# Second layer's experts: both parts of the tokens as 128 stationary columns in the gate and up products

## The chip, the cores and the metric

The kernel runs on one core of one Trainium2 chip. The metric is the device time of one launch in microseconds (us), as a median of several runs. The engines are named as the profile names them: PE (TensorE, matmuls), PEld (its loads of the stationary operand), DVE (VectorE), ACT (ScalarE), POOL (GpSimd) and SP (SyncE, which issues most DMAs). Each engine executes its own queue of instructions in order.

## What is computed

The reference is a model of two layers on 256 context and 256 latent tokens of 1024 channels. In each layer four mixers run, their outputs are merged, and a mixture of 16 experts follows, of which each token uses two. The change touches only the experts of the second layer, which treats the 256 latent tokens alone:

```python
def moe_ffn(u, w_group, w_expert, w_gate, w_up, w_down):
    ...
    comb = jnp.sum(jax.nn.one_hot(e_idx, MOE_EXPERTS, dtype=F32) * top_w[..., None], axis=-2).astype(u.dtype)
    y = jnp.zeros_like(u)
    for e in range(MOE_EXPERTS):
        h = jax.nn.silu(u @ w_gate[e]) * (u @ w_up[e])
        y = y + comb[..., e:e + 1] * (h @ w_down[e])
    return y
```

`w_gate` and `w_up` are 1024 x 512 for each expert, `w_down` is 512 x 1024, all float32: 6.3 MB of weights for each of 16 experts.

## The kernel before

**Products in parts.** PE multiplies operands of a rounded float32 type at full speed, so each float32 operand of a large product is split into a high and a low part. `split` (line 298) makes the high part as a copy on ACT (line 299) and the low part as a difference on DVE (line 300). `mm3` (line 320) adds three products: high times high, high times low, low times high. `wsplit` (line 311) loads 1024 columns of weights (512 KB, a tile `raw`) and splits them into `wh` and `wl`. In the expert stage three pairs of buffers take the split weights in turn, so a cast to `wh` waits until PE has finished with the block three before it. The `raw` tiles are a ring of some 21 buffers that SP fills ahead.

**An expert** (`expert`, line 371) has 12 such blocks: four of the gate (`mg`), four of the up (`mup`), four of the down matrix (`mdn`). In the second layer its tokens, at most 64, lie in `xs`: high and low part, channels in partitions, gathered for four experts at a time by products with a selection (`gather`, line 595: tiles `pick`, `uh`, `ul`, result `xx`). For the gate and for the up product, 64 token columns are the stationary operand and 512 weight columns move: two times 24 matmuls. Then ACT takes a Tanh of the gate (line 1403) and DVE makes h in two steps (lines 1404 and 1405; called the first and the second step below). PE transposes h in four pieces (`tr`, line 331), and h is split into `hh` and `hl`. Then 24 matmuls with the down blocks give the output in two halves. ACT scales one half to `yo` (line 1417), DVE the other (line 1418), and POOL writes `yo` to the rows of Y2 in memory by an indirect DMA (line 1419; the trace calls the target Y).

**What is in flight.** The loop over experts is pipelined by generators: three gate blocks of expert e+1 are emitted, then the end of expert e (Tanh, h, transposes, down blocks, `yo`, the write), then the row list of expert e+2 (`entries`, line 1558), then the rest of e+1. `entries` picks the list by small products (`rent,pick`) and DVE puts it into `ri` and `rf` (lines 1575 and 1582). There are four buffers of `ri`, so from the fifth list on, writing `ri` waits until an earlier Y write, which reads its rows from that buffer, has landed. In the program as built that is the write of the `yo` just ahead of it in DVE's queue.

**What sets the order.** A scheduler orders the instructions of every engine when the program is built, by costs of its own. What DVE or PE executes next is therefore fixed, and a late operand stops all that stands behind it.

Of the kernel before, what the change touches and what calls it, by code (L numbers as in the profile page):

```python
# [22 lines left out]
KT = D // 128  # L23
HY0, S50, RW0, M20, GT0, NIN = 0, 768, 1024, 1984, 3016, 7112
# tiles of 128 columns of w_in: Hyena, S5, RWKV (r, k, v, wd | ad), Mamba (z, x, B, C), gates, then gd | dt
# [51 lines left out]
NQS = (2, 4)  # pairs of groups in a part of S5  # L77
# [3 lines left out]
# ---------------------------------------------------------------- constants of the shapes  # L81


def _cst():
# [16 lines left out]
    # N^T of two-token blocks, rows s, columns t; backward scans in partitions 0..63  # L101
# [15 lines left out]
    # places less 1024  # L117
# [3 lines left out]
    # a token's row in U, and in Y2 for its first and second expert; Y2's less that of the rows without a token  # L121
    c["tok"] = np.stack([tok + 1.0, tok, tok + 512.0, tok - 1024.0], 2).reshape(128, 16)
    # resets of the running sums at the ends of 64-token chunks
# [7 lines left out]
def _rows():  # L131
    """rows of the modulation in groups of 32 (context, latent; the bias in the first's third): to each token's stream, to latent"""
    half = np.r_[np.ones(64), np.zeros(64)]
    m = np.zeros((128, 2, 128))
    for p in range(0, 128, 32):
        m[p:p + 2, 0] = half, 1 - half
        m[p + 1, 1] = 1
    m[2] = 1
    return m.reshape(128, 256)
# [39 lines left out]
def pack(inp):  # L179
    """Lays the inputs out for the loads; no arithmetic on them."""  # L180
# [32 lines left out]
    # S5: rows (second index of a pair of groups, state), columns (part, direction, pair)  # L213
# [44 lines left out]
class K:  # L258
# [13 lines left out]
    def pool(self, es, name, bufs=1):  # L272
        """a pool on the side of the parts of a layer"""
        return es.enter_context(self.tc.tile_pool(name=name, bufs=bufs, side="right", reuse_waits="tile"))
# [4 lines left out]
    def stream(self, banks="abgabgab", weights="mggg", parts="mg"):  # L279
        """banks of PSUM and buffers of weights (as loaded, and in parts) that the following program takes in turn:  # L280
        parts of a layer that run beside each other have their own"""
        self.tags, self.wtags, self.ptags = banks, weights, parts or weights
        if RESET:
            self.turn = self.wturn = 0

    def banks(self, **n):
        """the banks of PSUM by tag"""
# [9 lines left out]
    # ---- float32 operands of the large products in two parts of 12 bits: a b = ah bh + al bh + ah bl  # L297
# [4 lines left out]
    def raw(self, ap):  # L302
        """1024 columns of weights"""
# [7 lines left out]
    def wsplit(self, ap, k):  # L311
        """the parts of 1024 columns of weights (k by 1024 / k)"""
# [18 lines left out]
    def tr(self, out, in_, base=0):  # L331
        """out = in_^T on the tensor engine"""
# [6 lines left out]
    def rsqrt(self, pool, out, x, tag):  # L339
        """out = x ** -0.5 by Newton's iteration from the exponent's half; x > 0, small tiles"""  # L340
# [11 lines left out]
    def proj(self, l, t, xm, c0, c1, n=128):  # L352
        """p^T of w_in's tile t: n columns in partitions, tokens c0..c1"""
# [6 lines left out]
    # ------------------------------------------------------------------ RWKV-7  # L360
    def rwkv(self, l, xm, pc, dtT, yT, ctx_out, beside):
        """yT[:, hp, :]: the mixer's output, channels in partitions; columns 0..255 context, 256.. latent.
        dtT: Mamba's dt, from the tile that has both's columns, with tokens in partitions"""
        v, s, g, c = self.v, self.s, self.g, self.c
        with ExitStack() as es:
# [23 lines left out]
            def shifted(ps, n, j, out):  # L389
                """p + (mean of its neighbours - p) mu"""  # L390
# [20 lines left out]
            lo = {0: 64, 1: 0}  # partitions of the solves  # L411
# [4 lines left out]
            own = {d: slice(lo[d], lo[d] + 64) for d in range(2)}  # columns of a direction in the pairs' matrices  # L416
# [8 lines left out]
            for hp in range(2):  # L425
# [3 lines left out]
                # kappa: k k_k over its norm in the head  # L429
# [7 lines left out]
                # block diagonal pairs, of directions or heads: -b~ and k~ against kappa~, and the solves' (later M)  # L437
# [5 lines left out]
                for st in range(2):  # L443
# [6 lines left out]
                    for d in range(2):  # L450
                        dh = 2 * d + hp
                        # decay in log, its running sum in each chunk, and W = exp of that
# [21 lines left out]
                        s.activation(cum, cum, AF.Exp, scale=-1.0)  # 1 / W  # L474
# [16 lines left out]
                        # products of a chunk's tokens, masked: rows k~ and b~ (b~ and k~ backward)  # L491
# [11 lines left out]
                    # (I - N)^-1 of every chunk, N = -tril(kappa~ beta~^T): pairs of blocks, doubling  # L503
# [8 lines left out]
                    def each(a, b, us=range(8)):  # L512
                        """a^T b of the pairs"""
# [18 lines left out]
                    # tokens in partitions: v above (below) the solves, kappa~, and [k~; -b~]  # L532
# [33 lines left out]
                    # per chunk: H' = W_T (M H + k~^T v - b~^T u0), and y's reading of H  # L566
# [15 lines left out]
                    # the states that chunks enter (block diagonal), the last one that of the next stream's first chunk  # L582
# [23 lines left out]
                    # y^T  # L606
# [10 lines left out]
                    # group norm over a head, bonus, gate  # L617
# [24 lines left out]
    def headscale(self, pool, sq, f, eps, is_max, ni):  # L642
        """(f * sum over a head of sq, with eps added or as its least) ** -0.5, over the head's partitions"""
# [18 lines left out]
    # ------------------------------------------------------------------ conv of three taps, channels in partitions  # L662
    def conv3(self, ps, out, w3, b, c0, c1):
        """ps holds columns c0..c1 (of one or both streams)"""
# [8 lines left out]
    def silu(self, x, t):  # L673
        """x = silu(x), with a scratch like it"""
# [4 lines left out]
    # ------------------------------------------------------------------ Mamba-2  # L679
    def mamba(self, es, l, xm, pc, yT, ctx_out, dtT):  # L680
# [4 lines left out]
        if True:  # L685
# [10 lines left out]
            # softplus = max(x, 0) + log1p(exp(-|x|)); log1p(e) = 2 atanh(e / (2 + e))  # L696
# [17 lines left out]
            # running sums within a stream: forward heads 0..3, backward 4..7  # L714
# [16 lines left out]
            # weights of the context's tokens in its last state  # L731
# [6 lines left out]
            for gr in range(2):  # L738
# [8 lines left out]
                # tokens in partitions  # L747
# [10 lines left out]
                # the context's last states, [n, (direction, head, p)]  # L758
# [11 lines left out]
                for st in range(0 if ctx_out else 1, 2):  # L770
                    # C B^T by pairs of tiles, rows j, columns i; masked for each direction
# [33 lines left out]
                # + d x  # L805
                v.scalar_tensor_tensor(yT[:, gr, y0:], X[:, y0:], col("md", gr), py[:, y0:], OP.mult, OP.add)
            # times silu(z), norm over the channels
# [28 lines left out]
    def sin_of(self, pool, out, x, tag, cos=None):  # L836
        """out = sin(x), cos = cos(x): x less its whole turns, taken off in three parts"""
# [20 lines left out]
    def exp_of(self, pool, out, x, tag):  # L858
        """out = exp(x) for small tiles: 2^k times a polynomial of the rest"""
# [13 lines left out]
        # 2^k in two factors  # L873
# [8 lines left out]
    # ------------------------------------------------------------------ Hyena  # L882
    def hyena_filter(self, l, pc, pool, H):
        """H: [frequency, tile, (cos, sin), channel] of the two-sided filters"""
# [87 lines left out]
    # ------------------------------------------------------------------ S5  # L972
    def s5_params(self, l, pool):
        """[state, (part, direction, pair)]: lambda_bar, (lambda_bar - 1) / lambda, the decay over a chunk of
        4 tokens, cos and sin of the angles of a token, and of 1, 2, .. 64 chunks"""
# [44 lines left out]
    def s5_setup(self, l, a, P, tmp, TM, F, TT, ct, R):  # L1020
        """Matrices of 4-token chunks of the pairs of part a: E tokens -> state at the chunk's end, F state that
        enters -> tokens, TT within the chunk; ct: turns of the state by chunk (cos, sin), R: its decay over a chunk."""
# [3 lines left out]
        if True:  # L1026
# [7 lines left out]
            def times(o, x, br, bi, n, conj):  # L1034
                """o = x * b, or the conjugate of (conjugate of x) * b; x, o: [.., re/im, ..]"""
# [927 lines left out]
```

## Time and profile before

| | |
|---|---|
| timed runs | median 2172.78 us (2167.97, 2172.78, 2173.02) |
| span of the profiled execution, first to last instruction | 2165.3 us (its time as a run is not recorded; the timed runs lie 2.7 to 7.7 us above the span) |
| busy, share of the span | PE 91%, PEld 69%, DVE 76%, ACT 46%, POOL 18% |
| mean granted clock of PE | 0.946 of 2.4 GHz |
| moved by DMA | 406.28 MB |
| second layer's experts | about 1836 to 2137 us |

Shares over the whole span say little here, because the kernel has stages with different limits. The stage of the change is read by itself: from the table of 20 us stretches, then from the waits, then from the instructions of DVE and PE in order of time. A matmul's length in the trace includes its way through the array; what a stream of them costs is the distance from start to start.

### The profile page before, as it was taken

What the parts mean: (1) busy time and instruction counts of PE and PEld (TensorE: products, weight loads), DVE (VectorE), ACT (ScalarE), POOL (GpSimd) and SP (SyncE); (2) the same over time, 40 slices, a digit from 0 to 9 for tenths busy, and PEclk for the clock granted to TensorE, in tenths of its full rate; (3) what the DMA queues carried; (4) which work ended last, traced back from release to release, by engine and by line L of the source; (5) the groups of instructions that cost most, each with busy time, mean ns of one, the idle gap of its engine ahead of it and who ended that gap; (6) DMA issues with size and microseconds to landing.
All of it is one profiled execution on the core that took longest, in us unless ns stands there. A gap on an engine that the chain in (4) does not pass through costs nothing. (4 is left out here: it accounts for less than half of the span.)

```text
span 2165.3 us, 31795 instructions
## 1 busy us (share of the span) xinstructions
PE 1970.2 (91%) x11290; PEld 1504.7 (69%) x11290; DVE 1651.0 (76%) x3451; ACT 985.5 (46%) x1571; POOL 399.0 (18%) x502
## 2 busy tenths in 40 slices
PE   6999999889999899999995899899798878999994
PEld 2779889567666678777774689897575767555652
DVE  5575675478888777999996686776879776888895
ACT  3321322244344234777773332323434335777783
POOL 1000100033532322102213010100524221010100
PEclk9999999889999898999998899999898988999997
DMA  7221221533444845999993221312434394899981
GB/s 299 78 74 59 74 67 52 197 123 113 156 146 154 313 172 186 362 368 372 372 341 138 84 90 63 98 52 76 160 134 161 129 350 174 304 329 366 330 325 64
DMA packets 131915, 406.28 MB, mean 188 GB/s; under 512 B 18139, under 2 KB 30205, under 8 KB 131361
## 3 DMA queue, kind: packets, MB, share of 16 engines
q1 hardware_dynamic: 125778, 388.34, 50.6%
q0 software_dynamic: 5968, 15.80, 2.3%
q8 instruction: 92, 1.51, 0.3%
q14 instruction: 77, 0.63, 0.1%
HBM read 374.72 MB, written 34.61 MB: 189 GB/s over the span
## 5 line engine op out<-in xcount | busy, mean ns | idle before, releaser
L299 ACT CAST wh<-raw 128x1024 fp32r<-128x1024 f32 x528 | 553.0, 1048 | 537.9 <-PE bank L337 482.9
L300 DVE TENSOR_TENSOR wl<-raw,wh 128x1024 fp32r<-128x1024 f32 x528 | 642.6, 1231 | 146.4 <-ACT wh L299 143.1
L337 PE MATMUL bank<-xmh,wh 128*128 128x512 f32 (+2 forms) x896 | 338.3, 378 | 15.8 <-ACT wh L299 14.7
L337 PE MATMUL bank<-xmh,wl 128*128 128x512 f32 (+2 forms) x896 | 331.0, 370 | 15.4 <-DVE wl L300 15.4
L337 PE MATMUL bank<-xml,wh 128*128 128x512 f32 (+2 forms) x896 | 326.4, 365 | 0.0
L337 PEld LDWEIGHTS bank<-xmh,wh 128*128 128x128 f32 (+1 forms) x896 | 176.7, 197 | 54.2 <-ACT wh L299 19.2
L337 PEld LDWEIGHTS bank<-xmh,wl 128*128 128x128 f32 (+1 forms) x896 | 175.9, 196 | 51.6 <-DVE wl L300 22.2
L337 PEld LDWEIGHTS bank<-xml,wh 128*128 128x128 f32 (+1 forms) x896 | 176.5, 197 | 29.2 <-issue 6.2
L337 PE MATMUL bank<-wh,xx 128*64 128x512 f32 x512 | 168.1, 397 | 0.2 <-ACT wh L299 0.2
L1419 POOL DMA_INDIRECT Y<-yo,ri x32 | 43.4, 1357 | 420.4 <-DVE yo L1418 304.8
L337 PE MATMUL bank<-DD,TB 128*128 128x64 f32 (+1 forms) x848 | 111.5, 273 | 1.3 <-DVE TB L523 0.9
L337 PEld LDWEIGHTS bank<-DD,TB 128*128 128x128 f32 x848 | 106.3, 192 | 6.0 <-DVE DD L598 0.9
L337 PE MATMUL bank<-wl,xx 128*64 128x512 f32 x256 | 102.8, 402 | 1.3 <-DVE wl L300 1.1
L337 PE MATMUL bank<-wl,hh 128*112 128x512 f32 (+1 forms) x256 | 99.9, 396 | 0.0
L337 PEld LDWEIGHTS bank<-wh,xx 128*64 128x64 f32 x512 | 69.6, 136 | 43.1 <-issue 1.4
L337 PE MATMUL bank<-wl,xh 128*112 128x512 f32 x240 | 97.9, 408 | 0.2
L337 PE MATMUL bank<-wh,hl 128*112 128x512 f32 (+1 forms) x256 | 97.4, 400 | 0.5 <-DVE hl L300 0.2
L337 PE MATMUL bank<-wh,xl 128*112 128x512 f32 x240 | 94.8, 395 | 0.9 <-DVE xl L300 0.9
L337 PE MATMUL bank<-wh,xh 128*112 128x512 f32 x240 | 92.8, 395 | 0.8 <-ACT xh L299 0.8
L337 PE MATMUL bank<-wh,hh 128*112 128x512 f32 (+1 forms) x256 | 89.8, 397 | 1.1 <-ACT hh L299 1.1
L337 PE MATMUL bank<-raw,c 128*32 128x256 f32 x768 | 71.3, 423 | 18.6 <-DMA raw<-in_modw_dram 18.6
L337 PE MATMUL bank<-DD,AB 128*128 128x64 f32 x640 | 84.5, 275 | 0.7 <-DVE DD L510 0.7
(547 smaller groups left out, 3799.5 us busy)
## 6 DMA issues: line engine op xcount, KB each, us to landing
raw<-in_mg_dram SPq DMA_DIRECT2D x128, 512.0 KB
raw<-in_mup_dram SPq DMA_DIRECT2D x128, 512.0 KB
raw<-in_mdn_dram SPq DMA_DIRECT2D x128, 512.0 KB
raw<-in_win_dram SPq DMA_DIRECT2D x112, 512.0 KB
raw<-in_modw_dram SPq DMA_DIRECT2D x96, 512.0 KB
GT<-t SPq DMA_DIRECT2D x32, 256.0 KB
raw<-in_wbr_dram SPq DMA_DIRECT2D x16, 512.0 KB
G<-GT SPq DMA_DIRECT2D x8, 1024.0 KB
```

What stands on the lines that cost most here:

```text
L299: self.s.copy(hi, src)
L300: (eng or self.v).tensor_tensor(lo, src, hi, OP.subtract)
L337: self.t.matmul(out, lhsT=lhsT, rhs=rhs, start=start, stop=stop)
L1419: g.indirect_dma_start(out=Y2, out_offset=bass.IndirectOffsetOnAxis(ap=to, axis=0), in_=yo, in_offset=None, bounds_check=1023, oob_is_err= ...
```

## The change

The two parts of the tokens' operand are stored side by side, so that for each block of 128 channels high and low part form one stationary operand of 128 columns. One product with `wh` then gives high times high in rows 0 to 63 of the bank and low times high in rows 64 to 127; a second one, of the high part alone with `wl`, adds high times low to rows 0 to 63. Two matmuls stand where three stood. ACT copies the two banks of gate and up to SBUF (`gu`), and PE multiplies each 128 x 128 piece of them with two stacked 64 x 64 identities (`i64`). That adds the two halves of rows and transposes in one step, and takes the place of the transposes: eight products for four transposes. Tanh and the two steps on h then run on 128 partitions x 256 columns in place of 64 x 512. The first layer and the overflow loop keep the old path. The diff also drops comments, so line numbers move: 1403 to 1405 become 1423 to 1425, 1418 becomes 1444, 1419 becomes 1445, 1575 and 1582 become 1601 and 1608, and line 1418 of the changed kernel is the new copy.

```diff
+        stacked = OC[l] and xs is not None
...
-        pg, pu = self.bank()[0:cap], self.bank()[0:cap]
+        hh, hl = (tmp.tile([128, 4, cap], F32R, tag="h" + x, bufs=xb[2], name="h" + x) for x in "hl")
+        pg, pu = self.bank(), self.bank()
         for nm, ps in (("mg", pg), ("mup", pu)):
             for kc in range(4):
                 wh, wl = weights(nm, kc, 2)
                 for k in range(2):
                     kk = 2 * kc + k
-                    self.mm3(ps, [z[:, kk] for z in xs], (wh[:, k], wl[:, k]), kk == 0, kk == KT - 1)
+                    if stacked:
+
+                        both = lambda: self.mm(ps, xs[:, kk], wh[:, k], kk == 0, kk == KT - 1)
+                        if kk < KT - 1:
+                            both()
+                        self.mm(ps[0:cap], xs[:, kk, 0:cap], wl[:, k], False, False)
+                        if kk == KT - 1:
+                            both()
+                    else:
+                        self.mm3(ps[0:cap], [z[:, kk] for z in xs], (wh[:, k], wl[:, k]), kk == 0, kk == KT - 1)
                 yield
...
+        if stacked:
+
+            pt = self.bank()
+            for j, ps in enumerate((pg, pu)):
+                r = tmp.tile([128, 512], F32, tag=f"gu{j}", bufs=1, name="gu")
+                s.copy(r, ps)
+                for k in range(4):
+                    self.mm(pt[:, 256 * j + 64 * k:256 * j + 64 * k + 64], r[:, 128 * k:128 * k + 128], self.c["i64"])
+            pg, pu = pt[:, 0:256], pt[:, 256:512]
+            h = tmp.tile([128, 256], F32, tag="h", bufs=xb[1], name="h")
+            s.activation(h, pg, AF.Tanh, scale=0.5)
+            v.scalar_tensor_tensor(h, h, 1.0, pg, OP.add, OP.mult)
+            v.scalar_tensor_tensor(h, h, 0.5, pu, OP.mult, OP.mult)
+            self.split(h.rearrange("p (k t) -> p k t", k=4), hh, hl)
+        else:
...
-                    xx = [tmp.tile([128, KT, 2, 128], F32R, tag="xx", bufs=3, name="xx") for _ in range(2)]
+                    xx = [tmp.tile([128, KT, 2, 2, 64], F32R, tag="xx", bufs=3, name="xx") for _ in range(2)]
...
-                        xs.append([xx[j // 2][:, :, z, 64 * (j % 2):64 * (j % 2) + 64] for z in range(2)])
+                        xs.append(xx[j // 2][:, :, j % 2].rearrange("p k z t -> p k (z t)"))
...
-                            s.copy(xx[j][:, k], ps.rearrange("p (z j t) -> p j z t", z=2, j=2)[:, j])
+                            s.copy(xx[j][:, k], ps.rearrange("p (z j i t) -> p j i z t", z=2, j=2, i=2)[:, j])
```

The scheduler writes the stage in another order with this. DVE, one loop of the middle of the stage, before; `wl` is the low part of a block of weights, `h` the two steps, `yo` the scaled half of the output:

```order
L1418 TENSOR_SCALAR yo<-bank,rf 64x512
L300 TENSOR_TENSOR wl<-raw,wh 128x1024 x2
L1404 SCALAR_TENSOR_TENSOR h<-h,bank 64x512
L300 TENSOR_TENSOR wl<-raw,wh 128x1024 x3
L1405 SCALAR_TENSOR_TENSOR h<-h,bank 64x512
L300 TENSOR_TENSOR wl<-raw,wh 128x1024 x2
L1575 TENSOR_SCALAR ri<-bank 64x1
L1582 COPY rf<-bank 64x1
L300 TENSOR_TENSOR wl<-raw,wh 128x1024
L300 TENSOR_TENSOR hl<-bank,hh 128x256
L300 TENSOR_TENSOR wl<-raw,wh 128x1024 x4
L1418 TENSOR_SCALAR yo<-bank,rf 64x512
```

The same place in DVE's queue in the changed kernel:

```order
L1444 TENSOR_SCALAR yo<-bank,rf 64x512
L300 TENSOR_TENSOR wl<-raw,wh 128x1024 x4
L1601 TENSOR_SCALAR ri<-bank 64x1
L1608 COPY rf<-bank 64x1
L300 TENSOR_TENSOR wl<-raw,wh 128x1024 x4
L1424 SCALAR_TENSOR_TENSOR h<-h,bank 128x256
L300 TENSOR_TENSOR wl<-raw,wh 128x1024
L1425 SCALAR_TENSOR_TENSOR h<-h,bank 128x256
L300 TENSOR_TENSOR hl<-h,hh 128x256
L300 TENSOR_TENSOR wl<-raw,wh 128x1024 x3
L1444 TENSOR_SCALAR yo<-bank,rf 64x512
```

Twelve subtractions stand in each loop both times. The two steps on h moved from the second, fourth and following places to the end, directly ahead of `hl`; three subtractions in place of four stand between `hl` and `yo`; and `ri` moved ahead. Between `yo` and `ri` there are 5, 3, 4, 4, 5, 4, 4, 4, 5, 3, 4 and 4 subtractions in the first twelve loops of the changed kernel, and no `ri` stands in the last three. In before `ri` stands after five subtractions and both steps in the first loop, after 2, 3 and 4 subtractions and the first step in the next three, and from there on ever later, behind the second step.

PE at the transposes of an expert in before (`cst,h`), followed by products of the next expert (`xx`) and the first down products (`hh`, `hl`):

```order
L337 MATMUL bank<-wh,xx 64x512 x2
L334 MATMUL bank<-cst,h 128x64 x4
L337 MATMUL bank<-wl,xx 64x512
L337 MATMUL bank<-wh,xx 64x512 x2
L337 MATMUL bank<-wl,xx 64x512
L337 MATMUL bank<-wh,xx 64x512
L337 MATMUL bank<-wh,hh 64x512 x2
L337 MATMUL bank<-wl,hh 64x512 x2
L337 MATMUL bank<-wh,hl 64x512 x2
```

And at the second four products with `gu` of an expert in the changed kernel:

```order
L337 MATMUL bank<-wl,xx 64x512
L337 MATMUL bank<-wh,xx 128x512
L337 MATMUL bank<-cst,gu 128x64 x4
L337 MATMUL bank<-wl,xx 64x512
L337 MATMUL bank<-wh,xx 128x512
L337 MATMUL bank<-wl,xx 64x512
L337 MATMUL bank<-wh,hh 64x512
L337 MATMUL bank<-wl,hh 64x512
L337 MATMUL bank<-wh,hh 64x512
L337 MATMUL bank<-wl,hh 64x512
L337 MATMUL bank<-wh,hl 64x512 x2
```

Five matmuls stood between the transposes and the first `hh` product; three stand between the last `gu` products and it now, while Tanh, both steps on h and the cast to `hh` come between them on ACT and DVE. SP's and POOL's queues keep their order.

## Rows read from the trace of the kernel before

**Rows 1.** 20 us stretches: length, busy per engine (instructions), granted clock, DMA share, GB/s.

```profile
1900.00:1920.00 20.00, 18.05 (x74) 9.90 (x73) 14.90 (x17) 12.54 (x15) 0.55 (x1) 0.91 0.85 295
...
2060.00:2080.00 20.00, 20.00 (x89) 11.23 (x88) 18.79 (x22) 15.54 (x19) 1.16 (x1) 1.00 1.01 389
```

**Rows 2.** Waits, 1740 to 2140: engine, line, releaser; total us, times, longest.

```profile
ACT wh L299 <- PE bank L337: 74.9, 115, 4.5
...
DVE ri L1575 <- DMA Y<-yo,ri: 8.2, 4, 3.1
```

**Rows 3.** Groups by shape, 1740 to 2140: busy us, mean ns; idle before.

```profile
L300 DVE TENSOR_TENSOR wl<-raw,wh 128x1024 fp32r<-128x1024 f32 x206 | 248.3, 1221 | 48.7 <-ACT wh L299 47.1 <-SPq L1650 0.2
...
L299 ACT CAST wh<-raw 128x1024 fp32r<-128x1024 f32 x206 | 215.5, 1048 | 92.2 <-PE bank L337 74.9 <-DMA raw<-in_wbr_dram 6.3 <-DMA raw<-in_mdn_dram 2.6
...
L1404 DVE SCALAR_TENSOR_TENSOR h<-h,bank 64x512 f32<-64x512 f32 x16 | 10.7, 671 | 0.0
...
L1318 DVE SCALAR_TENSOR_TENSOR G<-G,bank 128x256 f32<-128x256 f32 x24 | 8.9, 406 | 0.1
...
L1447 ACT COPY at<-bank 128x512 f32<-128x512 f32 x6 | 3.4, 586 | 2.7 <-PE bank L337 1.5 <-PE bank L334 1.1
```

**Rows 4.** Groups by shape, PE, whole run.

```profile
L337 PE MATMUL bank<-DD,TB 128*128 128x64 f32 x640 | 82.2, 271 | 0.9 <-DVE TB L523 0.9
```

**Rows 5.** DVE in time order, an undisturbed loop: start, length, line, tile, idle before.

```profile
1993.40 0.74 DVE L1418 TENSOR_SCALAR yo<-bank,rf 64x512 f32<-64x512 f32 x1
...
1997.01 3.48 DVE L300 TENSOR_TENSOR wl<-raw,wh 128x1024 fp32r<-128x1024 f32 x3
...
2011.14 0.73 DVE L1418 TENSOR_SCALAR yo<-bank,rf 64x512 f32<-64x512 f32 x1
```

**Rows 6.** Line 1418 (`yo`): count, ns, first and last start.

```profile
L1418 DVE TENSOR_SCALAR yo<-bank,rf x16: 734/736/742, 1854.8 to 2135.2; 64x512 f32<-64x512 f32 x16
```

**Rows 7.** DVE in time order, a loop that waits for the Y write.

```profile
1874.83 0.74 DVE L1418 TENSOR_SCALAR yo<-bank,rf 64x512 f32<-64x512 f32 x1
...
1881.92 0.15 DVE L1575 TENSOR_SCALAR ri<-bank 64x1 int32<-64x1 f32 x1 [3.09 <-DMA Y<-yo,ri]
...
1890.07 0.41 DVE L300 TENSOR_TENSOR hl<-bank,hh 128x256 fp32r<-128x256 f32 x1
...
1896.24 0.73 DVE L1418 TENSOR_SCALAR yo<-bank,rf 64x512 f32<-64x512 f32 x1
...
1903.81 0.15 DVE L1575 TENSOR_SCALAR ri<-bank 64x1 int32<-64x1 f32 x1 [2.77 <-DMA Y<-yo,ri]
```

**Rows 8.** PE in time order, from two windows.

```profile
1889.33 0.62 PE L337 MATMUL bank<-wh,hh 128*64 128x512 f32 x2
...
1904.08 0.51 PE L337 MATMUL bank<-pick,uh 128*128 128x256 f32 x2 [1.56 <-DVE rf L1582]
...
1906.52 1.05 PE L337 MATMUL bank<-wh,xx 128*64 128x512 f32 x2
...
1907.37 0.63 PE L337 MATMUL bank<-wl,xx 128*64 128x512 f32 x1
...
1967.13 0.46 PE L334 MATMUL bank<-cst,h 64*128 64x64 f32 x4
...
1967.52 0.44 PE L337 MATMUL bank<-wl,xx 128*64 128x512 f32 x1
...
1970.58 0.39 PE L337 MATMUL bank<-wh,hh 128*64 128x512 f32 x1
...
1970.81 0.40 PE L337 MATMUL bank<-wl,hh 128*64 128x512 f32 x1
```

**Rows 9.** A Y write's issue on POOL; landings of writes issued from 1876, from 2103.

```profile
1876.33 1.56 POOL L1419 DMA_INDIRECT Y<-yo,ri  x1 [18.83 <-ACT wh L299]
...
DMA to landing us min/median/max: 5.6/5.6/5.6
...
DMA to landing us min/median/max: 3.0/3.0/3.0
```

More of the change, by code (lines that the diff above doesn't have):

```diff
@@ L1399, in expert @@
                     kk = 2 * kc + k
-                    self.mm3(ps, [z[:, kk] for z in xs], (wh[:, k], wl[:, k]), kk == 0, kk == KT - 1)
-                yield
-        h = tmp.tile([128, 512], F32, tag="h", bufs=xb[1], name="h")[0:cap]
-        s.activation(h, pg, AF.Tanh, scale=0.5)
-        v.scalar_tensor_tensor(h, h, 1.0, pg, OP.add, OP.mult)
-        v.scalar_tensor_tensor(h, h, 0.5, pu, OP.mult, OP.mult)
-        ps = self.bank()
-        for k in range(4):
-            self.tr(ps[:, cap * k:cap * k + cap], h[:, 128 * k:128 * k + 128])
@@ L1409, in expert @@
-        hh, hl = (tmp.tile([128, 4, cap], F32R, tag="h" + x, bufs=xb[2], name="h" + x) for x in "hl")
-        self.split(ps[:, 0:4 * cap].rearrange("p (k t) -> p k t", k=4), hh, hl)
+                    if stacked:
[7 more added lines that the diff above has]
+                        self.mm3(ps[0:cap], [z[:, kk] for z in xs], (wh[:, k], wl[:, k]), kk == 0, kk == KT - 1)
@@ new lines, in expert @@
+                yield
+        if stacked:
[12 more added lines that the diff above has]
+        else:
+            pg, pu = pg[0:cap], pu[0:cap]
+            h = tmp.tile([128, 512], F32, tag="h", bufs=xb[1], name="h")[0:cap]
+            s.activation(h, pg, AF.Tanh, scale=0.5)
+            v.scalar_tensor_tensor(h, h, 1.0, pg, OP.add, OP.mult)
+            v.scalar_tensor_tensor(h, h, 0.5, pu, OP.mult, OP.mult)
+            ps = self.bank()
+            for k in range(4):
+                self.tr(ps[:, cap * k:cap * k + cap], h[:, 128 * k:128 * k + 128])
+            self.split(ps[:, 0:4 * cap].rearrange("p (k t) -> p k t", k=4), hh, hl)
```

## The prediction

> **What bounds the kernel now.** I read the table of 20 us stretches first. In the second layer's experts the matmuls fill the stretch (20.00 of 20 us at a granted clock of 1.00 in 2060 to 2080), DVE is busy 18.79, ACT 15.54, and the DMA share is 1.01 [rows 1]. So four things are close to full, and the waits must say which leads: ACT waits 74.9 us for PE to give back a buffer of split weights, 115 times [rows 2]. The matmuls start 0.23 us apart with nothing between them [rows 8]. PE leads. From one scaling of an output half on DVE (`yo`) to the next is 17.74 us [rows 5]; 72 matmuls of 0.229 us are 16.5 of it, and four transposes and the list products fill the rest. From the first `yo` (1854.8) to the last (2135.2) the stage takes 280.4 us [rows 6], 15 loops of 18.7 us: some carry the gather of four experts, and in the early ones DVE stood still at `ri`, four times, 8.2 us [rows 2].
>
> **The change, by work.** PE loses 16 of 72 matmuls in each expert, 16 x 0.229 = 3.7 us. It gains eight products for four transposes. The four took 0.39 us to the start of the next matmul [rows 8], so eight are 0.8 us at that pace, and 2.2 us if each cost the 0.271 us that one of the same form takes alone [rows 4]; in a stream they overlap, so I take 0.9 us. PE then needs 17.3 - 3.7 + 0.5 = 14.1 us. DVE's two steps on h go from 0.671 to about 0.41 us each [rows 3], 0.5 us less: 12 subtractions at a spacing of 1.13 us (one takes 1.22 [rows 3], three in a row 3.48 [rows 5]), 0.67 for `yo`, 0.33 for `hl`, 0.66 for h and 0.2 of small things make 15.4 us. ACT gains two copies of 0.586 us [rows 3] and saves 0.2 us in its Tanh; with 12 casts of 1.05 us or a little less back to back [rows 3] that is some 14 to 15 us. By work alone a loop could fall to 15.5 or 16 us. Stationary columns that grow from 64 to 128 load behind the matmul before and cost nothing; if that cover failed, 16 loads would add about 1 us to PE, which then has 1.5 us to spare.
>
> **The change, by order.** The engines execute in the order written, and that order moved more than the work did. In before, DVE runs yo, 2 wl, first step on h, 3 wl, second step, 3 wl, hl, 4 wl, yo: seven subtractions and hl stand between the second step and the next `yo`. After the transposes PE has five more matmuls to run while ACT and DVE make hh and hl. In the changed kernel DVE runs yo, 4 wl, ri, 4 wl, first step, wl, second step, hl, 3 wl, yo. Both steps have slid to the end of the loop, right ahead of the down products that wait for them, and `ri` now stands four subtractions behind `yo`. I add the loop up along that chain.
>
> (a) `yo` to `ri`. `ri` overwrites the row list of the Y write that this same `yo` starts. In two loops of before where `ri` came early it started 7.09 us after `yo` (1874.83 to 1881.92, 3.09 us of it idle) and 7.57 us after (1896.24 to 1903.81) [rows 7]. The write itself took 5.6 us from issue to landing [rows 9]. DVE's own work up to `ri` is 0.67 + 4 x 1.13 = 5.2 us, some 5.7 with ACT's casts in the way. So 7.1 us, between 5.7 (no wait) and 7.6.
>
> (b) `ri` to the second step: 0.14 + 4 x 1.13 + 0.33 + 1.13 = 6.1 us; ACT is ahead by its buffers, I allow 0.1 us more, 6.2.
>
> (c) Second step (0.41), cast to hh (0.37), hand-overs (0.1): 0.9 us. PE has only three matmuls behind the last products of gu, and they were done 3 us earlier.
>
> (d) First matmul of hh to `yo`: 6.9 us, as in before from 1889.33 [rows 8] to 1896.24 [rows 7]. It is 24 matmuls and, at their end, a cast and a subtraction that need a buffer back from the third block. DVE has four instructions here, 3.7 us of work, and waits for the rest.
>
> A loop is then 7.1 + 6.2 + 0.9 + 6.9 = 21.1 us, and 19.7 without the wait at `ri`. The same sum for before (0.67 + 8 x 1.13 + 2 x 0.6 = 10.9 us to hl, then 6.2 us from hl at 1890.07 to `yo` at 1896.24 [rows 7]) gives 17.1, against 17.74 measured [rows 5]. So PE's saving turns into idle time.
>
> The 15 loops, by what stands in each: seven of 21.1 make 147.7. Two have `ri` after three subtractions (22.2, one with a selection of 0.6 us more): 45. Three have `ri` after five, one subtraction less on the chain and most of the gather's 16 casts on ACT: 18.8 and about 1.2, so 60. Two without `ri`: 39. The last, shorter: 14.6. Sum 306.3 us against 280.4: **+25.9 us**.
>
> **TensorE's clock** is the unknown price. In before PE stood idle 1.56 us ahead of 1904.08, and soon after, matmuls started 0.43 us apart instead of 0.23 (three from 1906.52 to 1907.37) [rows 8]; the granted clock of 1900 to 1920 is 0.91, so part of it ran at 1.2 GHz and not at 2.4 [rows 1]. In the new order PE idles about 3 us ahead of the down products in each loop without a gather, 11 loops. The nearest fall lasted eight matmuls, 8 x 0.2 = 1.6 us lost if all of them are down products, none if they fall in time that is idle anyway. I take the middle, 0.8 us, 11 x 0.8 = +8.8 us (0 to 17.6). The Trainium skill, "TensorE: Matmul & The Clock Gate", section "Why this matters for your kernels", names gaps in PE's work as what takes the clock down; the rows at 1904 agree, and by that rule the upper end would hold.
>
> What precedes the first `yo` has the same chain and stays within 1 us; what follows the last is unchanged. The sum is made against the span, 2165.3 us; the median of the timed runs, 2172.78, lies 7.5 us above it, and I carry that over: 2172.8 + 25.9 + 8.8 = 2207 us.
>
> **The rivals.** *PE's work decides, and the kernel becomes faster.* For it: PE leads in before, and the casts wait for PE. If the chain had slack, loops would fall to DVE's 15.4 us and 3% of stalls, 15.9, with about 16.5 in the six loops that share a gather: 242 us, 38 less, **2135 us**. It decides if the second step is ready so early that PE never waits for hh; the written order of DVE speaks against that, since nine subtractions stand between `yo` and the second step whatever PE does. Chance 0.16. *`ri` does not wait.* With DMA less loaded than in before, the Y write could land sooner: it took 3.0 us when the weight stream had ended [rows 9]. Then `yo`, the 0.75 us to the issue on POOL (1875.57 to 1876.33) and the write are 0.74 + 0.75 + 3.0 = 4.5 us, under 5.7; the seven loops are 19.7 each, the two odd ones about as long, and all 15 together 290 us; with PE at full clock +9 or, with the small terms of (b) and (c) at their lower ends, +4 us: **2179 us**, slower by little or the same. The trace speaks against it: a write issued at 1876.33 with less than full DMA traffic took 5.6 us. The Trainium skill, "DMA: Bandwidth & Descriptors", section "Anatomy of one DMA", gives a fixed 2.0 us and bytes at 436 GB/s; for 256 KB that is an estimate of 2.6 us, which agrees with the 3.0 us at the end but not with the 5.6 us beside the weight loads. By the page the time would be this rival's. Chance 0.15. *The clock falls in every loop* and stays low through most of the down products: +26 and +18 or more, **2217 to 2230 us**. Chance 0.14. That the change does not do what it says is no rival: the new order holds 32 matmuls with xx for each expert, half of them with 128 columns, where 48 stood.
>
> **How the numbers follow.** Forecast (2190 to 2217) 0.55, the three rivals 0.16, 0.15 and 0.14. A measurement of this kernel can tell about 0.3%, 6.5 us. Faster by more than that: 0.16 from the first rival and 0.01 from the second. Within it: 0.10 from the second. Slower: 0.04 from the second, 0.55 and 0.14. The range leaves out the first rival and a little above: 2172 to 2230.
>
> **What the changed profile would show.** From `yo` to `yo` 19 to 22 us in place of 17.7; DVE idle at `ri` for the Y write in about ten loops, 1 to 2 us each; DVE idle at `yo` for PE, about 2 us in each loop; PE idle ahead of the first hh matmul, 2 to 3.5 us; DMA below 330 GB/s in the stage; a granted clock under 1.00. The prediction is wrong if the loops are 16 to 17 us with DVE without idle time, or if PE still leads at 20.00 of 20 at full clock.

## The result, and the profile after

The changed kernel takes 2273.64 us (2268.93 to 2275.98), the kernel before 2171.07 us in the runs beside it. The ratio is 1.0465, with a 95% interval of 1.0448 to 1.0482: slower by some 103 us, where +34 us were forecast and 2230 us was the upper end of the range. The profiled execution spans 2270.7 us, 105.4 us more than before. The loss lies where the change is: the first `yo` starts at 1859.44 us, 4.7 us later than in before (in the other runs below it lies between 1849.6 and 1864.4), the last one at 2240.30 us, so that 15 loops take 380.9 us in place of 280.4 [rows 6], and the end takes as long as it did.

Stretches of 20 us of the stage in the changed kernel (length; busy us and instructions of PE, PEld, DVE, ACT, POOL; granted clock, DMA share, GB/s), as in [rows 1]:

```profile
2000.00:2020.00 20.00, 16.37 (x58) 9.79 (x59) 13.78 (x16) 11.41 (x14) 2.77 (x1) 0.74 0.68 232
2020.00:2040.00 20.00, 11.82 (x46) 8.04 (x45) 8.24 (x11) 7.27 (x10) 1.80 (x1) 0.74 0.70 241
```

No engine is full any more. Where the matmuls filled 20.00 of 20 us, DVE was busy 18.79 and DMA 1.01 [rows 1], DVE is now busy 8 to 14, DMA is at 0.7 and part of the stretch runs at the lower clock of 1.2 GHz. Something is waited for in a ring. The waits of 1840 to 2260 us (engine, line, releaser; us in all, times, longest) say for what:

```profile
ACT wh L299 <- PE bank L337: 95.1, 74, 5.6
DVE wl L300 <- ACT wh L299: 78.9, 63, 3.6
DVE ri L1601 <- DMA Y<-yo,ri: 59.3, 12, 7.2
...
PE bank L337 <- ACT hh L299: 39.0, 13, 3.8
PE bank L337 <- DVE rf L1608: 33.3, 10, 5.9
```

The third row was 8.2 us in four waits [rows 2]. It is now 59.3 us in twelve, and it carries the fifth with it: PE needs the bank from which `rf` is read, and `rf` stands behind `ri` on DVE. One loop of DVE in order of time (start, length, line, tile; in brackets the idle time before and its releaser), to be held against [rows 5]:

```profile
2015.72 0.74 DVE L1444 TENSOR_SCALAR yo<-bank,rf 64x512 f32<-64x512 f32 x1
2016.38 4.61 DVE L300 TENSOR_TENSOR wl<-raw,wh 128x1024 fp32r<-128x1024 f32 x4
2027.60 0.15 DVE L1601 TENSOR_SCALAR ri<-bank 64x1 int32<-64x1 f32 x1 [6.60 <-DMA Y<-yo,ri]
...
2032.91 0.42 DVE L1424 SCALAR_TENSOR_TENSOR h<-h,bank 128x256 f32<-128x256 f32 x1 [0.46 <-ACT h L1423]
...
2035.18 0.41 DVE L1425 SCALAR_TENSOR_TENSOR h<-h,bank 128x256 f32<-128x256 f32 x1
...
2040.07 1.22 DVE L300 TENSOR_TENSOR wl<-raw,wh 128x1024 fp32r<-128x1024 f32 x1 [3.58 <-ACT wh L299]
...
2044.10 0.74 DVE L1444 TENSOR_SCALAR yo<-bank,rf 64x512 f32<-64x512 f32 x1
```

From `yo` to `ri` are 11.88 us, of which 6.60 are idle; to the second step another 7.58; then 0.91 to the first product with `hh` and 8.01 to the next `yo`: 28.38 us, in a loop for which 21.1 were forecast. The order is the one forecast, and every link of the chain but the third is longer. The first is long because of what POOL shows. Its issues of the Y write in the changed kernel, a few of sixteen (start, length):

```profile
2017.23 4.57 POOL L1445 DMA_INDIRECT Y<-yo,ri  x1 [24.00 <-ACT wh L299]
...
2097.33 1.56 POOL L1445 DMA_INDIRECT Y<-yo,ri  x1 [19.28 <-ACT wh L299]
...
2180.78 5.70 POOL L1445 DMA_INDIRECT Y<-yo,ri  x1 [25.03 <-ACT wh L299]
```

The issue at 2017.23 ends at 2021.80, 0.81 us after the end of DVE's run of four subtractions (2016.38 + 4.61 = 20.99), and the write lands 5.8 us after that. Most lengths in the two kernels go in steps of 1.13 us, the spacing of subtractions: 1.16, 2.30, 3.44, 4.57, 5.70; those of 1.56 to 1.60 stand where DVE itself began its first subtraction 0.3 us late. In before most issues took 1.16 us, as the first of these two. There the second subtraction waited a moment for its cast: it began 1.20 us behind the first (at 1995.26), not 1.13, and the issue ended 0.79 us after that, still beside this subtraction. In the second, DVE had two subtractions without a gap and then the first step on h (start 2014.07):

```profile
1994.89 1.16 POOL L1419 DMA_INDIRECT Y<-yo,ri  x1 [16.45 <-DVE yo L1418]
2012.63 2.30 POOL L1419 DMA_INDIRECT Y<-yo,ri  x1 [16.58 <-DVE yo L1418]
```

DVE's two subtractions there, the pause seen as 0.08 us more in all:

```profile
1994.07 2.42 DVE L300 TENSOR_TENSOR wl<-raw,wh 128x1024 fp32r<-128x1024 f32 x2
...
2011.81 2.34 DVE L300 TENSOR_TENSOR wl<-raw,wh 128x1024 fp32r<-128x1024 f32 x2
```

So POOL gets its issue done only where DVE's run of subtractions is broken, and a pause of 0.06 us breaks it. In the changed kernel ACT's casts lie ready behind `yo` (the last of the four ended at 2019.41, its subtraction began at 2019.78), so the run has no pause. In the loops with four subtractions it ends at `ri`, which waits for the very write: of the write only the issue that is held up lies beside DVE's work.

### The profile page after: what moved, and what is told of

It reads as the page before. It is cut to its first block, busy times and chain, and to the rows that moved or that the text cites. A ratio compares the mean times of both kernels' runs of the same rounds, so it can differ in the third digit from the quotient of the medians.

```text
span 2270.7 us, 31689 instructions
## 1 busy us (share of the span) xinstructions
PE 1983.4 (87%) x11226; PEld 1532.2 (67%) x11226; DVE 1644.9 (72%) x3451; ACT 995.5 (44%) x1603; POOL 436.1 (19%) x502
## 5 line engine op out<-in xcount | busy, mean ns | idle before, releaser
L1445 POOL DMA_INDIRECT Y<-yo,ri x32 | 80.2, 2506 | 485.7 <-ACT wh L299 369.5
L337 PE MATMUL bank<-wh,hh 128*112 128x512 f32 (+1 forms) x256 | 104.4, 439 | 39.6 <-ACT hh L299 39.6
L337 PE MATMUL bank<-wl,hh 128*112 128x512 f32 (+1 forms) x256 | 111.1, 434 | 0.0
L337 PE MATMUL bank<-wh,hl 128*112 128x512 f32 (+1 forms) x256 | 105.4, 433 | 0.3 <-DVE hl L300 0.2
L337 PE MATMUL bank<-wh,xx 128*128 128x512 f32 x256 | 102.0, 415 | 0.0
L337 PEld LDWEIGHTS bank<-wh,hh 128*112 128x112 f32 (+1 forms) x256 | 43.5, 170 | 69.7 <-ACT hh L299 47.4
```

The costliest lines, as they stand in the source:

```text
L337: self.t.matmul(out, lhsT=lhsT, rhs=rhs, start=start, stop=stop)
L1445: g.indirect_dma_start(out=Y2, out_offset=bass.IndirectOffsetOnAxis(ap=to, axis=0), in_=yo, in_offset=None, bounds_check=1023, oob_is_err= ...
```

## The experiments

Two theories stood after the result. A: the wait for the Y write is most of the loss. B: the late steps and PE's clock are, and the wait only fills time that would be idle anyway.

**The wait taken away.** With 16 buffers for the lists no list overwrites one that a write still reads; the steps on h keep their late places. (The scheduler then also sets the lists of four experts together.)

```diff
-                    ri = tmp.tile([128, 2], I32, tag="ri", bufs=4, name="ri")[0:cap]
-                    rf = tmp.tile([128, 1], F32, tag="rf", bufs=4, name="rf")[0:cap]
+                    ri = tmp.tile([128, 2], I32, tag="ri", bufs=16 if OC[l] else 4, name="ri")[0:cap]
+                    rf = tmp.tile([128, 1], F32, tag="rf", bufs=16 if OC[l] else 4, name="rf")[0:cap]
```

> The changed kernel with 16 buffers of the row lists (ri, rf) in the second layer in place of 4, nothing else: no list overwrites one that a Y write still reads. In the changed kernel the 15 loops from the first to the last yo take 380.9 us, 280.4 in before, and DVE stands still at ri for 59.3 us. Theory A (the wait for the Y write, which POOL issues only when DVE's run of subtractions ends, is most of the loss): loops fall from 25 to 29 us to 19.5 to 21.5, the stage to about 300 to 320 us, the time to 2190 to 2215. Theory B (the two steps on h that stand late in DVE's order, with PE idle behind them and its clock down, are most of the loss, and the wait only fills time that would be idle anyway): the time stays above 2230. Both say that it stays slower than before.

Measured: 2213.65 us, ratio 1.0217 (1.0188 to 1.0246); 319.4 us from the first to the last `yo`, 61.5 less than in the changed kernel, about the 59.3 us that DVE had stood at `ri`. B falls as the main cause. The loops without a gather take 21.1 to 22.8 us, and one 19.6, most of them more than A had said. What is left over before, 39 us, lies in the rest of the chain that the forecast had added up, as one loop of DVE and PE shows:

```profile
2095.65 0.74 DVE L1444 TENSOR_SCALAR yo<-bank,rf 64x512 f32<-64x512 f32 x1
2096.31 5.75 DVE L300 TENSOR_TENSOR wl<-raw,wh 128x1024 fp32r<-128x1024 f32 x5
...
2107.92 0.41 DVE L1425 SCALAR_TENSOR_TENSOR h<-h,bank 128x256 f32<-128x256 f32 x1
...
2117.06 0.74 DVE L1444 TENSOR_SCALAR yo<-bank,rf 64x512 f32<-64x512 f32 x1
```

```profile
2108.82 0.44 PE L337 MATMUL bank<-wh,hh 128*64 128x512 f32 x1 [3.76 <-ACT hh L299]
...
2111.15 0.63 PE L337 MATMUL bank<-wh,hh 128*64 128x512 f32 x1
2111.58 0.63 PE L337 MATMUL bank<-wl,hh 128*64 128x512 f32 x1
```

The second step stands 12.27 us behind `yo`; PE idles 3.76 us ahead of `hh`, starts its next products 0.43 us apart, and needs 8.24 us from there to `yo`.

**The same buffers in the kernel before**, as a control.

> The kernel before with 16 buffers of the row lists in the second layer: a control for the buffers alone. DVE stood still 8.2 us at ri in before. Theory A: those 8.2 us and some of PE's idle time in 1880 to 1920 go, 4 to 8 us less than before, about 2165. Theory B: within 3 us of before, since PE leads there.

Measured: 2163.47 us, ratio 0.998 (0.9968 to 0.9991), a stage of 273.6 us, 6.8 us shorter. The wait that cost the changed kernel 61 us cost the kernel before 7.

**What holds POOL's issue.** First, a copy of one element per partition behind each subtraction, to break the run:

```diff
-            return self.wsplit(ap, k)
+            w = self.wsplit(ap, k)
+            if OC[l] and xs is not None:
+                scr = tmp.tile([128, 1], F32, tag="scr", bufs=1, name="scr")
+                v.tensor_copy(scr[0:64], w[1][0:64, 0, 0:1])
+            return w
```

> The changed kernel with a copy of one element per partition (64x1, from the fresh wl) on DVE behind each of the 12 subtractions of an expert; the four row-list buffers stay. It breaks the runs of subtractions that read two operands from SBUF. In the changed kernel POOL's issue of the Y write lasts 0.02 + n x 1.135 us with n up to 5 (3.43, 4.57, 5.70), n counting the subtractions left in DVE's run. If it is the unbroken run that holds POOL's issue, it falls to 0.9 to 2.3 us, and ri starts 8 to 9.5 us behind yo in place of 11 to 12. If POOL's issue is long for another reason (more DMA in flight, a longer list), it stays at 3.4 to 4.6 us. The twelve copies cost DVE 1 to 2 us a loop, so the time itself says little: 2250 to 2290.

Measured: 2274.73 us, issues of 3.5 us in most loops. By the letter that is the other reading, but the rows show why it decides nothing:

```profile
2019.47 2.34 DVE L300 TENSOR_TENSOR wl<-raw,wh 128x1024 fp32r<-128x1024 f32 x2
2021.73 0.13 DVE L1380 COPY scr<-wl 64x1 f32<-64x1 f32 x1
2021.80 1.20 DVE L300 TENSOR_TENSOR wl<-raw,wh 128x1024 fp32r<-128x1024 f32 x1
2022.93 0.14 DVE L1380 COPY scr<-wl 64x1 f32<-64x1 f32 x1
```

```profile
2020.25 3.56 POOL L1449 DMA_INDIRECT Y<-yo,ri  x1 [23.90 <-ACT wh L299]
```

The issue ends at 2023.81, 0.88 us after the last copy starts, and the copy in the middle did not let it finish. Shortness alone doesn't explain that: in before and in the run with filler products below, pauses of 0.03 to 0.07 us were enough (a subtraction that began 1.16 to 1.21 us behind the one ahead of it). Whether this copy, which reads and writes SBUF, holds POOL too, or DVE has to stand still for a moment, this run can't tell. So the next probe put something long there that reads one operand from SBUF:

```diff
+PROBE = (("mup", 1),)
...
+            if OC[l] and xs is not None and (nm, kc) in PROBE:
+                scr = tmp.tile([128, 2], F32, tag="scr", bufs=1, name="scr")
+                v.tensor_reduce(scr[:, 0:1], w[1].rearrange("p k n -> p (k n)").bitcast(F32), AX.X, OP.add)
```

> The changed kernel (four row-list buffers) with one more DVE instruction in each expert: a sum over the 1024 columns of one wl (128x1024 to 128x1, one operand from SBUF, about 1.1 us), behind the second subtraction after yo. DVE's run behind yo is then two subtractions, the sum, one or two subtractions, ri. If a subtraction, with its two operands in SBUF, is what holds POOL's issue, the issue ends inside the sum: 1.2 to 2.4 us long, where the changed kernel has 3.4 to 5.7, and ri starts 9 to 10 us behind yo. If any unbroken run of DVE holds it, the issue lasts 4.5 us or more and ri starts 11 to 12.5 us behind yo.

DVE and POOL in one loop:

```profile
2010.87 0.74 DVE L1449 TENSOR_SCALAR yo<-bank,rf 64x512 f32<-64x512 f32 x1
2011.53 2.34 DVE L301 TENSOR_TENSOR wl<-raw,wh 128x1024 fp32r<-128x1024 f32 x2
2013.80 1.20 DVE L1381 TENSOR_REDUCE scr<-wl 128x1 f32<-128x1024 f32 x1
2014.93 1.21 DVE L301 TENSOR_TENSOR wl<-raw,wh 128x1024 fp32r<-128x1024 f32 x1
2020.18 0.15 DVE L1606 TENSOR_SCALAR ri<-bank 64x1 int32<-64x1 f32 x1 [4.05 <-DMA Y<-yo,ri]
```

```profile
2012.38 2.30 POOL L1450 DMA_INDIRECT Y<-yo,ri  x1 [25.34 <-ACT wh L300]
```

The issue ends 0.88 us after the sum starts, inside an unbroken run of DVE. All issues but the last, which takes 0.90, are 1.57 to 2.31 us long, none 3.4 or more, and `ri` starts 7.2 to 9.3 us behind `yo`, a little sooner than expected. The kernel takes 2254.36 us, some 19 less than the changed kernel although DVE has 1.1 us more to do in each expert (a single run, and not timed beside the changed kernel); the stage takes 357.4 us, 23.5 less. So it is the subtraction with its two operands in SBUF that holds POOL. A DVE instruction with one lets it go where it is long enough, as the sum here and, in before, the first step on h (0.67 us, the other operand in a bank); the copy of one element did not.

The Trainium skill has this rule: "SBUF — State Buffer", section "Who interferes with whom", says that a DVE instruction with two SBUF inputs contends with a GpSimd instruction that reads SBUF, and that a reduction never does. The issue lengths of 4.57 and 2.30 us agree. The page has the lock held for one instruction; here four subtractions in a row held it four times as long. The same section says that a `tensor_tensor` did not stall a DMA in a probe, and infers why; here the subtraction, which is a `tensor_tensor`, held up the issue of one. In both the measurement decides.

**The clock.** With 16 buffers, twelve products without a use behind those of `gu`, in PE's idle time:

```diff
+FILL = 12
...
+            for k in range(FILL):
+                self.mm(pu[0:cap], xs[:, k % KT, 0:cap], xs[:, 4 * (k % 2):4 * (k % 2) + 4])
             pg, pu = pt[:, 0:256], pt[:, 256:512]
```

> As the run with 16 row-list buffers alone (2213.65 us, 319.4 us from first to last yo), with 12 more products of 64x512 on PE in each expert, behind the last products of gu, on a bank that is no longer read: they fill PE's idle time ahead of the down products and change no result. There, 11 of 15 loops take 8.0 to 9.3 us from the first product with hh to yo, 6.7 us in before, and PE starts some of these products 0.43 us apart. If it is PE's clock, fallen in the idle time, that makes them slow, the filled kernel shows a granted clock of 0.97 or more in the stage and 6.7 to 7.2 us from hh to yo, 15 to 25 us less in the stage; the order that the scheduler writes with it also sets the two steps one subtraction earlier in most loops (up to 1.1 us each). Time 2175 to 2195. If the products are slow because they wait for casts and buffers, hh to yo stays at 8 us or more and the time above 2200.

Measured: 2194.95 us, ratio 1.012 (1.0103 to 1.0137); the stage 304.1 us, 15.3 less. A stretch of it, and PE at the down products:

```profile
2100.00:2120.00 20.00, 18.00 (x84) 11.07 (x83) 15.59 (x17) 14.10 (x17) 2.30 (x1) 1.00 0.89 319
```

```profile
2118.67 2.96 PE L338 MATMUL bank<-xx 128*64 128x512 f32 x12
...
2123.53 0.45 PE L338 MATMUL bank<-wh,hh 128*64 128x512 f32 x1 [1.21 <-ACT hh L300]
2123.81 0.39 PE L338 MATMUL bank<-wl,hh 128*64 128x512 f32 x1
```

The granted clock is 1.00 all through the stage, and from `hh` to `yo` are 7.0 us, as in before. From `yo` to `hh` they are 13.36 us in the loop shown (`yo` at 2110.17), against 13.17 in the one without the filler: the other order of the steps gave nothing. Over the eleven loops without a gather, `hh` to `yo` falls by 17.6 us and `yo` to `hh` grows by 4.2. So the 15 us are the clock's, and the kernel does 12 more products in each expert to win them. The time is at the upper end of what was expected, and still above that of the kernel before.

**The order.** The same products, emitted in three pieces, so that the gate's fold, Tanh and first step come behind the first up block, and the up half's fold and second step behind the first gate block of the next expert (`fold` is the copy `gu` and its four products; the run has the 16 buffers):

```diff
+GE, UE = 0, 1
...
+                if stacked and nm == "mup" and kc == GE:
+                    pt = self.bank()
+                    fold(0, pg)
...
+                    v.scalar_tensor_tensor(h, h, 1.0, pt[:, 0:256], OP.add, OP.mult)
                 yield
+            fold(1, pu)
+            v.scalar_tensor_tensor(h, h, 0.5, pt[:, 256:512], OP.mult, OP.mult)
+            self.split(h.rearrange("p (k t) -> p k t", k=4), hh, hl)
+            yield
...
+                        if OC[l] and j == UE:
+                            next(prev, None)
```

> The changed kernel with 16 row-list buffers, and the end of an expert emitted in three pieces: the copy and four products of the gate with Tanh and the first step behind the first up block, those of up with the second step and the split behind the first gate block of the next expert, the down products where they were. DVE's order is then yo, 3 wl, first step, 3 wl, second step, 2 wl, hl, 4 wl, yo. If the late steps and the wait are all that is wrong with the changed kernel (A and B together), a loop goes to DVE's 15.5 to 16 us or the 16.1 us that 6.3 MB take at 390 GB/s, with 1 us for gathers: 240 to 255 us for 15 loops, the time 2130 to 2150, faster than before. If the stacked products cost more than was reckoned (loads of 128 columns, eight products with gu, two more copies on ACT), loops stay at 17.5 us or more and the time at 2170 or above.

Measured: 2149.09 us, ratio 0.9905 (0.9879 to 0.9931), faster than before by 1%; the stage takes 265.3 us, above the 240 to 255 expected. A loop of DVE:

```profile
2056.83 0.74 DVE L1449 TENSOR_SCALAR yo<-bank,rf 64x512 f32<-64x512 f32 x1
2057.49 3.71 DVE L301 TENSOR_TENSOR wl<-raw,wh 128x1024 fp32r<-128x1024 f32 x3
2061.12 0.41 DVE L1425 SCALAR_TENSOR_TENSOR h<-h,bank 128x256 f32<-128x256 f32 x1
...
2064.97 0.41 DVE L1429 SCALAR_TENSOR_TENSOR h<-h,bank 128x256 f32<-128x256 f32 x1
...
2069.83 1.23 DVE L301 TENSOR_TENSOR wl<-raw,wh 128x1024 fp32r<-128x1024 f32 x1 [0.71 <-ACT wh L300]
...
2073.73 0.74 DVE L1449 TENSOR_SCALAR yo<-bank,rf 64x512 f32<-64x512 f32 x1
```

The second step is at 8.14 us behind `yo` in place of 12.27 or 19.46, and DVE hardly waits. With this order the stacked products bring the kernel forward by 14 us against the kernel before with the same buffers (2163.47 us), 8 of them in the stage (273.6 to 265.3). The loops are 16.90 us, not the 15.5 to 16.1 that were expected.

The same with the four buffers of before:

> The kernel with the early pieces (2149.09 us with 16 row-list buffers) with the four buffers of before and of the changed kernel, nothing else. DVE's order has the steps early, and ri behind the subtractions of a loop at ever later places, four to twelve instructions behind yo. If the wait costs only where ri stands closer behind yo than the write takes (1.5 us to the issue, 1 us of issue, 5.8 us of landing), one to three early loops lose 1 to 3 us each: 2149 to 2156. If a list that waits costs in every loop, ten loops of 3 us or more: above 2175, slower than before.

Measured: 2151.89 us, ratio 0.9927 (0.9911 to 0.9944). DVE stands at `ri` three times, 2.5 us in all. With the steps early the scheduler sets `ri` later and into a broken run, and the lists need no more buffers.

**What bounds the early kernel.** Loads halved for the down blocks:

```diff
+        if half:
+            self.load(t[:, 0:512], ap)
+            return t[:, 0:512].unsqueeze(1).to_broadcast([128, 2, 512])
```

> The early kernel (16 row-list buffers, 2149.09 us) with the loads of the down blocks halved: 512 of 1024 columns are loaded, and cast and subtraction read them twice, so that the output is another, with the same instructions on PE, DVE and ACT. An expert's 6.3 MB of weights become 5.2 MB. There, a loop without a gather takes 16.90 us, with the DMA share at 0.96 to 1.02. If the loads bound those loops, they fall to 15.5 to 16.2 us, the time to 2135 to 2142. If DVE and its hand-overs with ACT and PE bound them, they stay at 16.7 to 16.9 us and the time within 5 us.

Measured: 2152.58 us, ratio 0.9919 (0.9898 to 0.9939), with loops of 16.91 us at a DMA share of 0.88 (0.99 in the early kernel): the loads don't bound them. Then DVE's `yo` given to ACT (`YA = (0, 1)`):

> The early kernel (16 row-list buffers, 2149.09 us) with both halves of the output scaled on ACT: DVE loses its yo (0.74 us) in each expert, ACT gains one of 0.68 us. In the early kernel a loop without a gather takes 16.90 us, DVE is busy 18.8 of 20 us there, ACT 16.9, and halving the loads of the down blocks changed nothing. If DVE's queue bounds those loops, each falls by about 0.65 us to 16.2 to 16.4, 15 loops by 8 to 10 us, the time to 2138 to 2143. If the hand-over of split buffers from PE to ACT bounds them (ACT stands 1.24 us for PE behind each hl, DVE 0.7 us behind that), the loops stay at 16.7 to 17.3 us and the time within 4 us, or a little longer, since ACT's cast then comes later.

Measured: 2160.87 us, ratio 0.9949 (0.9932 to 0.9966), 12 us longer than the early kernel, some 7 of them in the stage (272.1 against 265.3), and more than either reading allowed. DVE and ACT there:

```profile
2061.64 1.23 DVE L301 TENSOR_TENSOR wl<-raw,wh 128x1024 fp32r<-128x1024 f32 x1 [1.07 <-ACT wh L300]
...
2074.06 1.23 DVE L301 TENSOR_TENSOR wl<-raw,wh 128x1024 fp32r<-128x1024 f32 x1 [0.72 <-ACT wh L300]
```

```profile
2060.00 0.67 ACT L1449 ACTIVATE yo<-bank,rf 64x512 f32<-64x512 f32 x1
2060.57 1.03 ACT L300 CAST wh<-raw 128x1024 fp32r<-128x1024 f32 x1
...
2072.98 1.05 ACT L300 CAST wh<-raw 128x1024 fp32r<-128x1024 f32 x1 [1.26 <-PE bank L338]
```

The scaling on ACT delays the next cast, and DVE waits 1.07 us for it, in a loop of 17.49 us. So it is not DVE's work alone that bounds the early kernel: the hand-over from PE (a buffer back) to ACT (a cast) to DVE (a subtraction) is part of it. That more split buffers would mend this was not tried.

## Why the prediction was wrong, step by step

The stage grew by 100.5 us where +34.7 were forecast (306.3 us by the chain and 8.8 for the clock, against 280.4). The runs divide it so: 61.5 us the wait at `ri` (380.9 to 319.4), 15.3 us the clock (319.4 to 304.1), and a remainder of 23.7 us (304.1 to 280.4), which is what the late steps cost less what the smaller work and the wait in before (6.8 us) give back. The early kernel, with the steps early and neither the wait nor the low clock, takes 265.3 us there, 38.8 less than the one with filler products.

**What held.** PE, with 3.7 us less to do, no longer leads; DVE's written order does. The chain named is the one that the trace shows: `yo`, `ri`, second step, `hh`, `yo`. Term (c) is right to 0.01 us. Without the wait the chain took 319.4 us. That the forecast's whole sum, 315 us with a wait in it, lies near is luck: without its wait the forecast has 290 us and 9 for the clock, 20 too few. The first rival, PE's work decides, fell with the order, as was said; with another order the early kernel shows what it was after, in part.

**Term (a) is the step that failed.** It put 7.1 us from `yo` to `ri`, 5.7 to 7.6, as if the write ran beside DVE's subtractions. Measured are 7.0 to 12.5 us, 10.6 on average over twelve loops: 3.5 us x 12 = 42 of the 66 us that were missed. The forecast is the loop at 1874.83 [rows 7]: 1.50 us from `yo` to the issue, 1.56 of issue [rows 9], 4.0 from its end to `ri`. In the changed kernel these are on average 1.50, 3.54 and 5.52 us. So 2.0 of the 3.5 us are the issue and 1.5 the landing.

The issue: DVE in the loop that the forecast took its price from, in before:

```profile
1875.89 2.36 DVE L300 TENSOR_TENSOR wl<-raw,wh 128x1024 fp32r<-128x1024 f32 x2 [0.32 <-ACT wh L299]
1878.17 0.67 DVE L1404 SCALAR_TENSOR_TENSOR h<-h,bank 64x512 f32<-64x512 f32 x1
```

DVE was waiting for ACT's casts there, and the issue ended at 1877.89 beside the second subtraction, ahead of the first step. The order of the changed kernel, quoted ahead of the prediction, has four subtractions there and nothing between; that their casts would lie ready, so that no pause breaks the run, the order doesn't show. The length of POOL's issue was in the trace as a variable (1.16, 1.56, 2.30 us) and was read as a constant.

The landing: 3.9 to 6.5 us from the end of the issue to `ri`, where the row used had 4.0. Why it was longer stays open. That loads in flight delay it is seen in the early kernel: with halved loads the median from issue to landing falls from 5.7 to 3.8 us. But the changed kernel moved fewer bytes per second there (232 and 241 GB/s in the stretches above). The price of the wait was thus taken from one row whose neighbours were not those of the new order.

**Term (b)** was 6.2 us; in the nine loops without a gather's casts it was 7.0 to 8.6, 11 us in all above what was forecast for them. In the loop shown the wait caused this too: PE stood for `rf`, then ran its products with `gu` at the lower clock, so that Tanh came late (0.46 us idle at the first step). Without the wait the second step is 12.27 us behind `yo`, where (a) at its lower end and (b) give 11.9. That it is the wait in all nine is not shown.

**Term (d) and the clock.** 6.9 us plus 0.8 were reckoned for eleven loops, and 7.9 to 9.5 measured, 8.75 on average; 20 us in all where 8.8 were taken and 17.6 were the upper end. The one fall of before lasted eight products; here, in a loop whose down products start at 2063.68, about fourteen of 24 start 0.43 us apart, and only then 0.23 (PE in the changed kernel):

```profile
2068.86 0.63 PE L337 MATMUL bank<-wh,hh 128*64 128x512 f32 x1
2069.29 0.61 PE L337 MATMUL bank<-wl,hh 128*64 128x512 f32 x1
2069.72 0.42 PE L337 MATMUL bank<-wh,hl 128*64 128x512 f32 x1
2069.97 0.39 PE L337 MATMUL bank<-wh,hh 128*64 128x512 f32 x1
```

The run with filler products shows the cause, and 15.3 us as its price when the wait is absent.

**Second rival.** "`ri` does not wait", 2179 us, fell: the wait was there in every loop that has a list behind `yo`, and longer; with less moved by DMA the write did not land sooner. Even with the wait taken away by buffers the kernel took 2213.65. **Third rival:** the clock did fall in twelve of the fifteen loops, but it explains a seventh of the loss (15.3 us by the filler run) to a fifth (20 us by term (d)).

**Small terms.** The eight products with `gu` cost 1.8 us an expert where 0.9 were taken. The trace shows each of them as two matmuls, 0.11 us apart: four products are eight matmuls and take 0.89 us (2057.94 to 2058.83 in the early kernel). It is hidden here, since PE has time. The stationary columns of 128 cost nothing that the spacing shows: products with `xx` start 0.23 us apart.

## What to carry over

When a change takes work off the leading engine, read the new order on the engine that comes next and put a price on each wait in its new place: a wait costs what stands directly ahead of it there, not what it cost where it stood. In this kernel POOL's issue of an indirect DMA was held up by an unbroken run of DVE instructions with two SBUF operands (4.57 us beside four), so nothing that waits for it belongs at the end of such a run. Whether a run is unbroken depends also on whether its operands lie ready. With the same four list buffers, emitting the same instructions in smaller pieces turned +103 us into -18 us (2151.89 against 2170.28).

## What the runs showed of the hardware

POOL's issue of a 64-row indirect write takes 0.90 to 0.99 us in all 16 experts of the run with `yo` on ACT, where DVE waits at that moment. Beside subtractions of 1.13 us spacing that follow `yo` at once it takes 0.02 us plus a whole number of them, up to 5.70 us, and it ends 0.8 to 0.9 us after the run breaks, about as long as an issue takes by itself. One row stands against this: in the run with 16 buffers alone, the issue at 1880.94 took 1.16 us beside two subtractions without a gap. A pause of 0.03 to 0.07 us breaks the run; a copy of one element, 0.07 us between two subtractions, doesn't; a sum of 1.2 us does, from its start.
